# Layer A's o projection by pairs of heads: products of 512 moving columns instead of 256

## The chip, the cores and the metric

The kernel runs on 1 core of a Trainium2 chip. The metric is the device time of one execution in microseconds (us); before the change its median is 2071.47 us over 3 runs (2068.67 to 2078.06).

## The reference, cut to what matters

A trunk of two layers on a residual stream x of 1024 tokens by 1024 values, all in float32. Layer A is an mLSTM mixer, layer B dilated sliding-window attention. The change touches one product of layer A, the output gate `o_pre`, a third of the input projection:

```python
xm, z, o_pre = jnp.split(x @ w_in, 3, axis=-1)           # each 1024 x 2048
xc = jax.nn.silu(causal_dwconv(xm, conv_w, conv_b))
q, k, v = headwise(xc, wq), headwise(xc, wk), headwise(xm, wv)
gates = jnp.concatenate([q, k, v], axis=-1) @ w_if + b_if # i_pre, f_pre: 4 + 4 per token
h_tilde = mlstm_chunkwise(q, k, v, i_pre, f_pre)          # 4 heads of 512
h = jax.nn.sigmoid(o_pre) * h_tilde
y = (groupnorm(h) * gn_g + skip * xc) * jax.nn.silu(z)
x = layer_norm(ALPHA * x + y @ w_out)
```

## The kernel before, in words

**Precision.** A float32 operand is split in a high part (a cast to fp32r on ScalarE, L92) and a low part (a subtraction, L93, on VectorE or the engine passed as `l_eng`). `mm3` (L95 to L99) forms a product from three matmuls: high by high, high by low, low by high.

**Strassen.** Layer A's projections are 2x2 block products in Strassen's form (a variant of Winograd) with seven products in place of eight. The operands of x, `x["11"]`, `x["12"]`, `x["22"]` and the sums `s1` to `s4`, are made once (`operands`) and kept as high and low parts in slots 0 to 7 and 12 to 31. The weights come as four quarters b11, b12, b22, b21 (`quarters`, L177), from which sums are made in place (L243, L247, L260, L261). Results are sums of PSUM banks (`plus` L224, `result` L230).

**The o projection** (`layer_a_project`, L556 to L577) runs `strassen_steps` once for each of four heads. With `tokens` given, the activations are the stationary operand (128x128, 128 tokens) and the weights move, 256 columns in each matmul: one head has 512 columns, half of it is a block. A set of results, 512 tokens by 256 columns, takes two banks, so the four sets a, b, c, d take all eight. Each product splits its quarter in two halves of 128x512 and runs 2 x 4 x 2 x 3 = 48 matmuls. The order in one head is a (b11 by x11), a again (b21 by x12), the sums b12 and b11, b (by s2), u2 = u2 + b, c (by s3), u3 = u2 + c, d (by s1), c again (by x22), d again (by s4). c may be added to only after u3 has read it. `sigmoid` takes the tanh of each finished result (L570) into slots 38 and 39 and stores it in DRAM (L572). For head 0 the subtractions and sums of the weights are on GpSimd (`V if hd else G`), for the others on VectorE.

**Slots.** All large buffers in SBUF are numbered slots of 128 x 4 KB; a `Ring` hands them out in turn, and whoever asks for a slot waits for the last user of its former tile. In the o projection raw weights use 34, 35, 32, 33; split pairs 36, 37, 8, 9, 49, 47; u2 and u3 use 10, 11.

**Around it.** Ahead come the streams of xm and the z gates (`gates`, L453 to L459), with `values` (L521 to L530). `gate_tables` stands ahead of the o projection in the program: the rows `gs` (slot 47) go through four sets of small matmuls (L598, L600; two banks in turn), are copied by ScalarE (L602), and a chain of row operations follows, mostly on VectorE (L607 to L637). `columns()` (L647 to L651) comes after head 0. Behind it, `layer_a_attend` begins with `prep_q` (L686 to L692: a product with a block matrix loaded from `dA` to slot 48, through banks 6 and 7, then a split), `prep_v` (loads of v and casts, L679 to L681) and scores (banks 4 and 5). The xc rows are loaded (L581) into the slots that the operands s2, s3, s1, s4 of x leave free.

**Order.** The program is written as a dataflow. A planner puts it into one queue for each engine beforehand, from its own estimates of durations and with the program's order as priority; on the chip each queue runs strictly in that order. Nearly all DMAs are issued from one queue, SyncE's (SP).

Of the kernel before, what the change touches and what calls it, by code (L numbers as in the profile page):

```python
# [13 lines left out]
AF = mybir.ActivationFunctionType  # L14
ALU = mybir.AluOpType
# [3 lines left out]
P = 128  # L19
# [41 lines left out]
class Kernel:  # L61
# [123 lines left out]
    def strassen_steps(self, raw, x, banks, dest, done, eng, tokens=None, mid=None, early=False, second=False):  # L185
# [99 lines left out]
        yield  # L285
        result(0, 1, u2, d)

    def rstd(self, x, n, tag):

        v = self.nc.vector  # L290
        y = self.t(self.cp, [P, n], tag=tag + "y", bufs=4)
        w = self.t(self.cp, [P, n], tag=tag + "w", bufs=4)
        v.tensor_scalar(y.bitcast(I32), x.bitcast(I32), 1, -1,
                        op0=ALU.logical_shift_right, op1=ALU.bitwise_xor)
        v.tensor_tensor(y.bitcast(I32), y.bitcast(I32), self.magic[:, 0:n].bitcast(I32), op=ALU.add)
        for _ in range(3):
            v.tensor_tensor(w, y, x, op=ALU.mult)
            v.scalar_tensor_tensor(w, w, -0.5, y, op0=ALU.mult, op1=ALU.mult)
            v.scalar_tensor_tensor(y, w, 1.5, y, op0=ALU.add, op1=ALU.mult)
        return y  # L300
# [104 lines left out]
    def layer_a_project(self):  # L405
        nc, tc, a, cp = self.nc, self.tc, self.a, self.cp
        V, A, G, T = nc.vector, nc.scalar, nc.gpsimd, nc.tensor
# [3 lines left out]
        def load(half, kh, js=range(2)):  # L411
            for j in js:
# [3 lines left out]
        x = self.operands(raws, {"11": (0, 1, 2, 3), "12": (4, 5, 6, 7), "22": (12, 13, 14, 15), "s1": (16, 17, 18, 19),  # L416
                                 "s2": (20, 21, 22, 23), "s3": (24, 25, 26, 27), "s4": (28, 29, 30, 31)}, {})
# [135 lines left out]
        columns = self.gate_tables(gs, gx, pv)  # L553


        self.w_raw, self.w_hl, self.u_slots = Ring(34, 35, 32, 33), Ring(36, 37, 8, 9, 49, 47), Ring(10, 11)  # L556
        tos = Ring(38, 39)
        for hd in range(HA):
            to = {}

            def place(half, i):
                to[half, i] = t = self.slot(tos, (P, 2, 512))
                return [[(t[:, j], slice(0, P))] for j in range(2)]

            def sigmoid(half, i, aps):
                if (half, i) == (0, 0):
                    place(0, 0)
                t = to[half, i]
                for j in range(2):
                    A.activation(t[:, j], aps[j], AF.Tanh, scale=0.5)  # L570
                rows = self.dram["o", hd].rearrange("(h t p) (i n) -> h i p t n", h=2, p=P, i=2)[half, i]
                nc.sync.dma_start(rows, t.rearrange("p j (t n) -> p (j t) n", t=2))  # L572

            self.strassen(self.quarters(a["w_o"][hd]), x, ((0, 1), (2, 3), (4, 5), (6, 7)), place, sigmoid, V if hd else G,
                          tokens=lambda ap, t: ap[:, t * P:t * P + P])
            if hd == 0:
                columns()  # L577
        self.xc = []
        for c in range(NC_A):
# [858 lines left out]
def arrays_of(i):  # L1438

    c = np.ascontiguousarray  # L1440
    x = np.asarray(i["x"])[0]
    w_in = np.asarray(i["a_w_in"])[0]
    kv = np.asarray(i["b_w_kv"])
    w2 = np.asarray(i["b_w_in"])[0]
    coltile = lambda w: c(w.reshape(KD, P, -1, P).transpose(2, 1, 0, 3)).reshape(-1, P, KD * P)
    perch = lambda v: c(v.reshape(NC_A, P).T)
    r = {"x": x, "ln_g": np.asarray(i["ln_g"]), "ln_b": np.asarray(i["ln_b"])}

    def quarters(w):
        t = w.reshape(-1, 2, P, 2, 512)  # L1450
        return c(np.stack([t[:, 0, :, 0], t[:, 1, :, 0], t[:, 1, :, 1], t[:, 0, :, 1]], 1).reshape(
            -1, 2, 2, P, 512).transpose(0, 1, 3, 2, 4)).reshape(-1, 2, P, 1024)

    r["lnT"] = c(np.stack([r["ln_g"][0].reshape(KD, P).T, r["ln_b"][0].reshape(KD, P).T], 1))
    r["xq"] = c(x.T.reshape(4, 2, P, 2, 512).transpose(3, 0, 2, 1, 4)).reshape(2, 4, P, 1024)
    r["w_xm"] = quarters(coltile(w_in[:, 0:INNER]))
    r["w_z"] = quarters(coltile(w_in[:, INNER:2 * INNER]))
    wo = w_in[:, 2 * INNER:].reshape(2, 4, P, HA, 2, 256).transpose(3, 0, 4, 2, 1, 5).reshape(HA, 2, 2, P, 1024)
    r["w_o"] = np.stack([wo[:, 0, 0], wo[:, 0, 1], wo[:, 1, 1], wo[:, 1, 0]], 1)
    r["convw"] = c(np.asarray(i["a_conv_w"])[0].reshape(4, NC_A, P).transpose(2, 1, 0))  # L1460
    r["convb"] = perch(np.asarray(i["a_conv_b"])[0])
    for n in ("q", "k", "v"):
        r[f"w{n}T"] = c(np.asarray(i["a_w" + n])[0].transpose(0, 2, 1).reshape(NC_A, P, 4).transpose(1, 0, 2))
    rep = lambda w: c(np.repeat(w[:, None], 4, axis=1).reshape(NC_A, P, *w.shape[1:]).swapaxes(0, 1))
    r["wkr"] = rep(np.asarray(i["a_wk"])[0])
    r["wifr"] = np.stack([rep(w) for w in np.asarray(i["a_w_if"])[0].reshape(3, 512, 4, 8)])
    r["bif"] = c(np.asarray(i["a_b_if"])[0].reshape(2, 4).T)
    r["gng"] = perch(np.asarray(i["a_gn_g"])[0])
    r["skip"] = perch(np.asarray(i["a_skip"])[0])
    r["w_out"] = c(np.asarray(i["a_w_out"])[0].reshape(NC_A, P, D))  # L1470
    kvt = kv.reshape(KD, P, 3, 2, HB, P)
    wv = kvt[:, :, :, 1].reshape(2, 4, P, 3, 2, 2, 256).transpose(3, 4, 0, 5, 2, 1, 6).reshape(3, 2, 2, 2, P, 1024)
    r["w_v2"] = quarters(kvt[:, :, 2, 1].transpose(2, 1, 0, 3)).reshape(2, 2, 2, P, 1024)
# [37 lines left out]
```

## Time and profile before

| | |
|---|---|
| median of 3 runs | 2071.47 us |
| profiled execution | 2070.5 us, span 2068.7 us |
| PE (TensorE) busy | 2001.8 us, 97% |
| PEld (weight loads) busy | 1721.8 us, 83% |
| DVE (VectorE) busy | 1462.1 us, 71% |
| ACT (ScalarE) busy | 1003.1 us, 48% |
| POOL (GpSimd) busy | 188.9 us, 9% |

Times of rows are us from the start of the span. A row of a timeline is start, duration, engine, line, operation, output from input with shapes, count of merged instructions, and in brackets the engine's idle time before it with what ended it. Matmuls are pipelined: their durations overlap, so the cost of one in a stream is the distance between starts. A row of groups (by line and form) ends with busy time, mean ns of one, then the idle time ahead of them and what ended it. In a table of windows the columns are the stretch, its length, the busy time (and instructions) of PE, PEld, DVE, ACT and POOL, the granted clock of PE, the busy share of the DMA engines and GB/s.

### The profile page before, as it was taken

How to read it: one execution, taken by the hardware profiler on the slowest of the kernel's cores; microseconds unless marked ns; L12 is line 12 of the kernel's file. 1: busy time of each engine (PE TensorE's matmuls, PEld its weight loads, DVE VectorE, ACT ScalarE, POOL GpSimd, SP SyncE). 2: the span in 40 equal slices, each digit the busy share in tenths (PEclk: the TensorE clock that was granted, in tenths of full speed). 3: DMA queues.
4: the chain of work that ended last, by engine and by line, in shares of the span. 5: the costliest groups of instructions: out<-in, count | busy, mean ns of one | idle time of the engine just before them, and what ended most of it. 6: DMA issues, size and time to landing. Idle time of an engine off the chain costs nothing.

```text
span 2068.7 us, 29452 instructions
## 1 busy us (share of the span) xinstructions
PE 2001.8 (97%) x11008; PEld 1721.8 (83%) x11008; DVE 1462.1 (71%) x2825; ACT 1003.1 (48%) x1920; POOL 188.9 (9%) x145
## 2 busy tenths in 40 slices
PE   8989999999999999999999999999999999999997
PEld 6868888899888888877788898888888898888786
DVE  8787788465367767465678757766878757757878
ACT  5455555533745453343434536555534635655631
POOL 0230000600244443000000000000000000000000
PEclk9999999999999999999999999999999999999999
DMA  4455555443844643516113231122543132123753
GB/s 166 145 190 175 181 214 175 153 146 114 324 172 158 214 146 114 199 62 213 56 46 127 68 133 62 61 93 91 187 166 121 64 113 70 62 92 106 260 210 122
DMA packets 117046, 288.20 MB, mean 139 GB/s; under 512 B 13028, under 2 KB 43172, under 8 KB 116904
## 3 DMA queue, kind: packets, MB, share of 16 engines
q1 hardware_dynamic: 116904, 286.34, 39.2%
q8 instruction: 86, 1.41, 0.3%
q14 instruction: 56, 0.46, 0.1%
HBM read 200.00 MB, written 86.30 MB: 138 GB/s over the span
## 4 chain that ended last, share of the span: by engine, by line
PE 77%; DVE 11%; DMA 7%; ACT 2%; issue 2%; SPq 0%; DVEq 0%; ACTq 0%
PE b L97 24%; PE b L99 24%; PE b L98 24%; DVE s L93 3%; DMA s<-df 3%; PE b L521 1%; PE b L1159 1%; DMA s<-dv 1%; DVE s L141 1%; ACT s L92 1%; PE b L527 1%; PE b L788 1%; DVE s L1276 1%; DVE s L486 1%; DVE s L230 0%
## 5 line engine op out<-in xcount | busy, mean ns | idle before, releaser
L97 PE MATMUL b<-s,s 128*128 128x512 f32 (+2 forms) x3256 | 1125.4, 354 | 28.4 <-ACT s L92 16.7
L98 PE MATMUL b<-s,s 128*128 128x512 f32 (+2 forms) x3256 | 1140.6, 352 | 9.3 <-DVE s L93 9.3
L99 PE MATMUL b<-s,s 128*128 128x512 f32 (+2 forms) x3256 | 1125.1, 352 | 5.3 <-DVE s L93 5.1
L97 PEld LDWEIGHTS b<-s,s 128*128 128x128 f32 x3256 | 617.0, 190 | 117.4 <-ACT s L92 22.3
L92 ACT CAST s<-s 128x512 fp32r<-128x512 f32 (+4 forms) x674 | 435.1, 659 | 552.9 <-PE b L99 318.3
L98 PEld LDWEIGHTS b<-s,s 128*128 128x128 f32 x3256 | 619.7, 190 | 88.1 <-DVE s L93 10.7
L99 PEld LDWEIGHTS b<-s,s 128*128 128x128 f32 x3256 | 617.9, 190 | 88.5 <-DVE s L93 8.4
L93 DVE TENSOR_TENSOR s<-s,s 128x512 fp32r<-128x512 f32 (+3 forms) x656 | 500.9, 773 | 248.0 <-ACT s L92 245.4
L230 DVE TENSOR_TENSOR s<-s,b 128x512 f32<-128x512 f32 x192 | 130.5, 682 | 70.8 <-PE b L99 61.5
L224 DVE TENSOR_TENSOR s<-s,b 128x512 f32<-128x512 f32 x128 | 86.5, 680 | 26.6 <-PE b L99 25.9
L1146 ACT ACTIVATE s<-s,nmax 128x128 f32<-128x128 f32 (+1 forms) x192 | 84.5, 442 | 38.3 <-DVE nmax L1144 37.5
L93 DVE TENSOR_TENSOR s<-b,s 128x512 fp32r<-128x512 f32 (+1 forms) x96 | 59.0, 630 | 43.3 <-ACT s L92 43.0
L486 DVE SCALAR_TENSOR_TENSOR s<-s,c_convw,s 128x512 f32<-128x512 f32 (+3 forms) x96 | 74.8, 786 | 2.3 <-ACT s L483 1.8
L1142 DVE CUSTOM_DVE_ANT_0 s<-b,k 128x128 f32<-128x128 f32 (+1 forms) x192 | 57.8, 345 | 17.5 <-PE b L99 17.4
L243 DVE TENSOR_TENSOR s<-s,s 128x512 f32<-128x512 f32 (+1 forms) x55 | 41.6, 756 | 39.3 <-DMA s<-in_w_xm 13.9
L722 ACT ACTIVATE s<-s,k 128x128 f32<-128x128 f32 x144 | 46.9, 392 | 41.7 <-DVE s L93 19.3
L92 ACT CAST s<-b 128x512 fp32r<-128x512 f32 (+1 forms) x96 | 50.3, 545 | 31.8 <-PE b L99 19.7
L681 POOL TENSOR_TENSOR s<-s 128x512 fp32r<-128x512 f32 x32 | 43.3, 1369 | 161.6 <-DMA s<-dv 112.4
L93 POOL TENSOR_TENSOR s<-s,s 128x512 fp32r<-128x512 f32 x18 | 30.5, 1702 | 254.1 <-ACT s L92 253.2
L237 ACT COPY s<-b 128x512 f32<-128x512 f32 x64 | 37.4, 585 | 26.0 <-PE b L99 25.6
L792 POOL TENSOR_TENSOR s<-s,s 128x512 f32<-128x512 f32 x32 | 42.3, 1338 | 62.8 <-DVE s L791 47.9
L1095 ACT ACTIVATE s<-s 128x512 fp32r<-128x512 f32 x48 | 42.0, 882 | 11.8 <-DVE s L230 11.6
(178 smaller groups left out, 1448.4 us busy)
## 6 DMA issues: line engine op xcount, KB each, us to landing
s<-in_w_qk SPq DMA_DIRECT2D x48, 512.0 KB
s<-in_w_out SPq DMA_DIRECT2D x40, 512.0 KB
dp<-s SPq DMA_DIRECT2D x32, 512.0 KB
s<-dp SPq DMA_DIRECT2D x32, 512.0 KB
s<-in_w_z SPq DMA_DIRECT2D x24, 512.0 KB
s<-in_w_v SPq DMA_DIRECT2D x24, 512.0 KB
dg<-s SPq DMA_DIRECT2D x24, 512.0 KB
s<-dg SPq DMA_DIRECT2D x24, 512.0 KB
```

The costliest lines, as they stand in the source:

```text
L92: self.nc.scalar.copy(h, src)
L93: (l_eng or self.nc.vector).tensor_tensor(l, src, f(h), op=ALU.subtract)
L97: mm(ps, lh, rh, start=start, stop=False, skip_group_check=skip)
L98: mm(ps, lh, rl, start=False, stop=False, skip_group_check=skip)
L99: mm(ps, ll, rh, start=False, stop=stop, skip_group_check=skip)
L224: V.tensor_tensor(o, p, q, op=add)
L230: V.tensor_tensor(o, p[lane][rows], q[lane][rows], op=add)
L486: V.scalar_tensor_tensor(u[i][:, lo:o + 512], xm[i][:, lo - s:o + 512 - s], convw[:, c, 3 - s:4 - s], u[i][:, lo:o + 512], op0=ALU.mult, o ...
L681: G.tensor_tensor(l, f(l), f(h), op=ALU.subtract)
L722: A.activation(E[:, i * P:i * P + P], src[:, i * P:i * P + P], AF.Exp, bias=self.bias[:, hd, ig, j:j + 1])
L1142: V.tensor_tensor_reduce(out=dst, in0=sc, in1=bias, op0=ALU.add, op1=ALU.max, scale=1.0, scalar=-3e38, accum_out=mx[:, b:b + 1])
L1146: A.activation(res[b][0], res[b][0], AF.Exp, bias=nm[:, b:b + 1], accum_out=stat[:, 1, g, b:b + 1])
```

## The change

A new function, `strassen_wide`, does the seven products for two heads at once: a block is now 512 columns, a whole head, and a set of results takes four banks (one for each 128 tokens). The eight banks hold two sets, so b takes 4 to 7 after a has taken 0 to 3, c 0 to 3 again, d 4 to 7. A quarter of the weights is two slots of 1024; each product makes four splits of 128x512, for each of which four matmul triples of 512 columns run. The split pairs are four (36, 37, 49, 47), the raw quarters have fixed places (pair 0: 34, 35, 50, 51, 32, 33, 48, 52), u2 and u3 use 8 to 11. VectorE does the subtractions and sums of both pairs. The weights in DRAM are laid out anew on the host.

```diff
+    def strassen_wide(self, raw, x, banks, dest, done, eng):
+        b11, b12, b22, b21 = raw
+        banks = Ring(*banks)
+        new = lambda: [self.bank(i) for i in banks.next()]
+        u2, u3 = [[t[:, j] for t in [self.slot(self.u_slots, (P, 2, 512)) for _ in range(2)] for j in range(2)]
+                  for _ in range(2)]
+        def product(acc, w, xp, first):
+            for k in range(4):
+                wh, wl = self.pair(self.w_hl)
+                self.split(wh, wl, w[k // 2][:, k % 2 * 512:k % 2 * 512 + 512], eng)
+                xh, xl = [p[k // 2][:, k % 2] for p in xp]
+                for t in range(4):
+                    ts = slice(t * P, t * P + P)
+                    self.mm3(acc[t], xh[:, ts], xl[:, ts], wh, wl, first and k == 0, k == 3, skip=True)
+        def sums(o, p, q, op):
+            for j in range(2):
+                eng.tensor_tensor(o[j], p[j], q[j], op=op)
...
+        a = new()
+        product(a, b11, x["11"], True)
+        for o, p in zip(u2, a):
+            A.copy(o, p)
+        product(a, b21, x["12"], False)
+        done(0, 0, a)
+        sums(b12, b22, b12, sub)
+        sums(b11, b12, b11, add)
+        b = new()
+        product(b, b11, x["s2"], True)
+        plus(u2, u2, b)
+        c = new()
+        product(c, b12, x["s3"], True)
+        plus(u3, u2, c)
+        sums(b21, b21, b11, sub)
+        sums(b11, b22, b11, sub)
+        d = new()
+        product(d, b11, x["s1"], True)
+        result(1, 1, u3, d)
+        product(c, b21, x["22"], False)
+        result(1, 0, u2, c)
+        product(d, b22, x["s4"], False)
+        result(0, 1, u2, d)
...
-        self.w_raw, self.w_hl, self.u_slots = Ring(34, 35, 32, 33), Ring(36, 37, 8, 9, 49, 47), Ring(10, 11)
+        self.w_hl, self.u_slots = Ring(36, 37, 49, 47), Ring(8, 9, 10, 11)
         tos = Ring(38, 39)
-        for hd in range(HA):
+        places = (((34, 35), (50, 51), (32, 33), (48, 52)), ((50, 51), (48, 52), (34, 35), (32, 33)))
+        for pair in range(2):
+            raw = {}
+            for n in (0, 3, 1, 2):
+                kh, nh = ((0, 0), (0, 1), (1, 1), (1, 0))[n]
+                raw[n] = [self.slot(i) for i in places[pair][n]]
+                for j in range(2):
+                    nc.sync.dma_start(raw[n][j], a["w_o"][pair, kh, nh, j])
...
-            self.strassen(self.quarters(a["w_o"][hd]), x, ((0, 1), (2, 3), (4, 5), (6, 7)), place, sigmoid, V if hd else G,
-                          tokens=lambda ap, t: ap[:, t * P:t * P + P])
-            if hd == 0:
+            self.strassen_wide([raw[n] for n in range(4)], x, ((0, 1, 2, 3), (4, 5, 6, 7)), place, sigmoid, V)
+            if pair == 0:
                 columns()
```

## Rows read from the trace of the kernel before

**Rows 1.** The page: engines' busy time, and the last chain by line.

```profile
PE 2001.8 (97%) x11008; PEld 1721.8 (83%) x11008; DVE 1462.1 (71%) x2825; ACT 1003.1 (48%) x1920; POOL 188.9 (9%) x145
PE b L97 24%; PE b L99 24%; PE b L98 24%; DVE s L93 3%; DMA s<-df 3%; PE b L521 1%; PE b L1159 1%; DMA s<-dv 1%; DVE s L141 1%; ACT s L92 1%; PE b L527 1%; PE b L788 1%; DVE s L1276 1%; DVE s L486 1%; DVE s L230 0%
```

**Rows 2.** Windows of the o projection and of the stretch behind it.

```profile
390.00:412.40 22.40, 22.40 (x190) 22.40 (x188) 18.98 (x14) 12.82 (x17) 17.83 (x9) 1.00 0.31 95
415.00:418.40 3.40, 3.17 (x15) 3.20 (x16) 3.40 (x7) 0.00 (x0) 0.00 (x0) 0.50 0.63 245
418.40:550.40 132.00, 132.00 (x1107) 131.85 (x1107) 68.40 (x99) 64.15 (x110) 7.00 (x5) 1.00 0.51 173
555.70:561.80 6.10, 6.10 (x15) 5.07 (x16) 2.05 (x3) 2.21 (x5) 3.30 (x3) 0.50 1.03 413
```

**Rows 3.** PE's timeline: narrow matmuls in the stage, wide ones later, first and last.

```profile
449.74 0.28 PE L98 MATMUL b<-s,s 128*128 128x256 f32 x1
...
451.90 0.28 PE L98 MATMUL b<-s,s 128*128 128x256 f32 x1
...
899.70 0.39 PE L98 MATMUL b<-s,s 128*128 128x512 f32 x1
...
901.97 0.39 PE L99 MATMUL b<-s,s 128*128 128x512 f32 x1
```

**Rows 4.** PE's timeline: its two stops, and the end of the half speed.

```profile
415.23 0.55 PE L97 MATMUL b<-s,s 128*128 128x256 f32 x1 [2.55 <-DVE s L224]
...
418.50 0.28 PE L97 MATMUL b<-s,s 128*128 128x256 f32 x1
...
555.70 1.54 PE L97 MATMUL b<-s,s 128*128 128x512 f32 x3 [3.72 <-ACT s L92]
```

**Rows 5.** Groups by line and form, 371 to 450 us: low parts of weights.

```profile
L93 POOL TENSOR_TENSOR s<-s,s 128x512 fp32r<-128x512 f32 x12 | 21.3, 1784 | 14.0 <-ACT s L92 13.7 <-DVE s L230 0.4
...
L93 DVE TENSOR_TENSOR s<-s,s 128x512 fp32r<-128x512 f32 x12 | 8.1, 684 | 9.1 <-ACT s L92 9.0
```

**Rows 6.** DVE's timeline from 389 us: gate chain and o work.

```profile
389.96 0.84 DVE L607 TENSOR_SCALAR s<-s 4x1024 f32<-4x1024 f32 x1 [12.07 <-ACT s L602]
390.83 3.31 DVE L608 TENSOR_TENSOR s<-s,s 4x1024 f32<-4x1024 f32 x1
...
396.70 2.20 DVE L612 TENSOR_TENSOR s<-s,s 4x1024 f32<-4x1024 f32 x1
...
407.97 3.27 DVE L623 TENSOR_TENSOR_SCAN s<-s,s 4x1024 f32<-4x1024 f32 x1
...
414.42 1.26 DVE L224 TENSOR_TENSOR s<-s,b 128x512 f32<-128x512 f32 x2
...
418.73 1.20 DVE L628 TENSOR_TENSOR s<-s,s 4x1024 f32<-4x1024 f32 x1
...
420.59 1.21 DVE L243 TENSOR_TENSOR s<-s,s 128x1024 f32<-128x1024 f32 x1
```

**Rows 7.** PE's timeline: end of the z gates, last set of gate matmuls.

```profile
374.68 0.48 PE L99 MATMUL b<-s,s 128*128 128x512 f32 x1
...
387.23 1.02 PE L598 MATMUL b<-s,c_sel 16*4 16x512 f32 x2
388.17 1.04 PE L600 MATMUL b<-c_ident,gx 128*4 128x128 f32 x8
```

**Rows 8.** ACT's timeline from 372 us: casts that waited for a slot or load.

```profile
376.79 0.62 ACT L92 CAST s<-s 128x512 fp32r<-128x512 f32 x1 [0.24 <-DMA dz<-s]
...
385.43 1.04 ACT L92 CAST s<-s 128x1024 fp32r<-128x1024 f32 x1 [0.81 <-DMA s<-in_w_out]
...
388.28 0.62 ACT L92 CAST s<-s 128x512 fp32r<-128x512 f32 x1 [1.22 <-PE b L598]
```

**Rows 9.** Timelines of DVE and of ACT at the stage's end.

```profile
552.38 1.28 DVE L230 TENSOR_TENSOR s<-s,b 128x512 f32<-128x512 f32 x2 [6.82 <-DMA do<-s]
...
552.99 0.62 ACT L680 CAST s<-s 128x512 fp32r<-128x512 f32 x1 [2.95 <-DMA s<-dv]
```

**Rows 10.** SP's timeline: loads of the xc rows.

```profile
527.46 9.44 SPq L581 DMA_DIRECT2D s<-dc  x8
```

More of the change, by code (lines that the diff above doesn't have):

```diff
@@ L286, in strassen_steps, with plus, result @@
         result(0, 1, u2, d)
+    def strassen_wide(self, raw, x, banks, dest, done, eng):
+        V, A = self.nc.vector, self.nc.scalar
+        sub, add = ALU.subtract, ALU.add
+        b11, b12, b22, b21 = raw
[14 more added lines that the diff above has]
+                eng.tensor_tensor(o[j], p[j], q[j], op=op)
+        def plus(outs, ps, qs):
+            for o, p, q in zip(outs, ps, qs):
+                V.tensor_tensor(o, p, q, op=add)
+        def result(half, i, p, q):
+            o = dest(half, i)
+            plus(o, p, q)
+            done(half, i, o)
+        a = new()
[21 more added lines that the diff above has]
+        result(0, 1, u2, d)
     def rstd(self, x, n, tag):
@@ L553, in layer_a_project @@
         columns = self.gate_tables(gs, gx, pv)
-        self.w_raw, self.w_hl, self.u_slots = Ring(34, 35, 32, 33), Ring(36, 37, 8, 9, 49, 47), Ring(10, 11)
+        self.w_hl, self.u_slots = Ring(36, 37, 49, 47), Ring(8, 9, 10, 11)
         tos = Ring(38, 39)
-        for hd in range(HA):
+        places = (((34, 35), (50, 51), (32, 33), (48, 52)), ((50, 51), (48, 52), (34, 35), (32, 33)))
[6 more added lines that the diff above has]
+                    nc.sync.dma_start(raw[n][j], a["w_o"][pair, kh, nh, j])
             to = {}
             def place(half, i):
-                to[half, i] = t = self.slot(tos, (P, 2, 512))
-                return [[(t[:, j], slice(0, P))] for j in range(2)]
+                to[half, i] = [self.slot(tos, (P, 2, 512)) for _ in range(2)]
+                return [t[:, j] for t in to[half, i] for j in range(2)]
             def sigmoid(half, i, aps):
@@ L567, in sigmoid @@
                     place(0, 0)
[L568 to L572, printed above, removed]
-            self.strassen(self.quarters(a["w_o"][hd]), x, ((0, 1), (2, 3), (4, 5), (6, 7)), place, sigmoid, V if hd else G,
-                          tokens=lambda ap, t: ap[:, t * P:t * P + P])
-            if hd == 0:
+                rows = self.dram["o", 2 * pair + i].rearrange("(h j t p) n -> h j p t n", h=2, j=2, p=P)
+                for j, t in enumerate(to[half, i]):
+                    for k in range(2):
+                        A.activation(t[:, k], aps[2 * j + k], AF.Tanh, scale=0.5)
+                    nc.sync.dma_start(rows[half, j], t)
+            self.strassen_wide([raw[n] for n in range(4)], x, ((0, 1, 2, 3), (4, 5, 6, 7)), place, sigmoid, V)
+            if pair == 0:
                 columns()
@@ L1457, in arrays_of @@
     r["w_z"] = quarters(coltile(w_in[:, INNER:2 * INNER]))
-    wo = w_in[:, 2 * INNER:].reshape(2, 4, P, HA, 2, 256).transpose(3, 0, 4, 2, 1, 5).reshape(HA, 2, 2, P, 1024)
-    r["w_o"] = np.stack([wo[:, 0, 0], wo[:, 0, 1], wo[:, 1, 1], wo[:, 1, 0]], 1)
+    r["w_o"] = c(w_in[:, 2 * INNER:].reshape(2, 2, 2, P, 2, 2, 512).transpose(4, 0, 5, 1, 3, 2, 6)).reshape(
+        2, 2, 2, 2, P, 1024)
     r["convw"] = c(np.asarray(i["a_conv_w"])[0].reshape(4, NC_A, P).transpose(2, 1, 0))
```

## Prediction

> **What bounds the kernel now.** I began with the busy line of the page and the shares of the last chain [rows 1]: TensorE (PE) is busy 97% of the span and the three matmul lines of `mm3` make up some 72% of the chain. So an edit is worth what it does to the matmul stream, plus or minus what makes that stream wait. The windows [rows 2] then cut out the o projection. It begins beside the last z-gate product, near 375 us, and ends at 550.4. For the heads after the first (418.4 to 550.4) PE and the weight-load row are both full, 132.00 and 131.85 of 132 us, with VectorE (DVE) at 68.40 and ScalarE (ACT) at 64.15: PE alone is the limit there. In the first head two other engines carry load: DVE works on the gate tables, GpSimd (POOL) on head 0's subtractions.
>
> Third, the matmul timeline gives the price of a product by its width [rows 3]. 128x256: 18 steps from 449.74 to 451.90 us, 0.120 us each. 128x512, the same three lines with activations stationary and weights moving as the change has them: 10 steps from 899.70 to 901.97, 0.227 us each. Two narrow products cost 0.240 us, one wide 0.227.
>
> Fourth, PE's stops [rows 4]. There are two in the stage or at its end. At 415.23 PE had been idle 2.55 us for DVE's L224, the sum u3 = u2 + c, without which the next product may not add into c. The next 15 matmuls take 3.27 us where 15 x 0.120 = 1.80 is normal, at a granted clock of 0.50 (the lower level, 1.2 GHz) [rows 2]: 1.5 us more. Cost of the first stop 2.6 + 1.5 = 4.1 us. At 555.70, in the first steps of the attention, PE had been idle 3.72 us for an ACT cast, and 6.1 us at 0.50 follow [rows 2, 4], which cost half of themselves if PE was the limit in them, 3.0 us. Together 6.7 us.
>
> **The change part by part.**
>
> *Width.* 4 heads x 7 products x 48 matmuls = 1344 of 256 columns become 2 x 7 x 48 = 672 of 512. 1344 x 0.120 = 161.3 us against 672 x 0.227 = 152.5: **-8.8 us**, nearly all of it on the path, since PE is full there. Only the reading of the steps leaves play: 8.5 to 9.2.
>
> At 256 columns the weight-load row is as full as PE's [rows 2]. The Trainium skill, "TensorE: Matmul & The Clock Gate", section Back-to-back issue gap, gives N/2.4 + 2.5 ns for an isolated step, 109.2 and 215.8 ns, and warns that loads also set the step in a real stream. By that formula the change would be worth 672 x 2.6 ns = 1.7 us; by the rows, five times that.
>
> *Work of the other engines.* Casts, subtractions and sums stay equal in number: 56 splits of 128x512 (4 per product instead of 2), 16 sums of 128x1024, 32 tanh, 16 loads and 16 stores of 512 KB. The stores now write rows of 512 values instead of 256, so the queue is not longer. One thing moves: head 0 used POOL for 14 subtractions and 4 sums; now DVE does them, 14 x 0.684 + 4 x 1.21 = 14.4 us [rows 5, 6]. For pair 1 (half of all o work) that is nothing: DVE needs some 28 x 0.69 + 8 x 1.21 + 20 x 0.68 = 42.6 us in a pair of 76.2 us (336 x 0.227). What matters is pair 0.
>
> *The gate chain beside pair 0.* DVE's queue is strictly in order. It stood idle 12.07 us before L607 at 389.96 [rows 6], waiting for ACT's L602, which itself waits for the fourth set of gate matmuls on PE [rows 7]. From 390.0 to 412.4 it was busy 18.98 us with 14 instructions, of which two were o work [rows 2]. In the changed kernel subtractions of pair 0 lie in that queue too, before, between and behind the chain. In favour: the 12 idle us lie just there; L608 took 3.31 us beside a busy POOL, L628 of the same form 1.20 with POOL idle [rows 6], so with POOL silent the chain loses at least 2.1 us; and the wait that cost 4.1 us (u3 before c is used again) now has a product of 48 x 0.227 = 10.9 us between instead of 48 x 0.120 = 5.8. Against: the ring of split pairs shrinks from six to four, a look-ahead of 4 x 12 x 0.227 = 10.9 us instead of 6 x 24 x 0.120 = 17.3. From 390.0 to 412.4 DVE had 22.4 - 18.98 = 3.4 us free, with the 2.1 some 5.5; in that time, two products, it must now place 8 subtractions and 4 sums, 8 x 0.684 + 4 x 1.21 = 10.3 us. What lacks, 4.8 us, must go into the idle 12 us ahead of L607 or into the look-ahead. If neither takes any, PE stands 4.8 us and loses 1.5 at half speed after it, so I bound the new stop by 0 and 6 and take 2, nearer to 0 because the idle time is over twice the lack: **-2.1 us**, with -4.1 and +1.9 as ends.
>
> *Slots at the start.* Three buffers come free late, and the rows show when. Pair slot 49 is released by the z store (the cast at 376.79 waited for it), slot 47 holds the gate rows and is released by the last L598 (the cast at 388.28 waited for that) [rows 8]. In the new ring of four these are the third and the fourth quarter of the very first product; before, they were the fifth and sixth pair. So the first product cannot end before about 389.4 (cast 0.62, then DVE). Does PE have other work until then? The last z-gate matmul starts at 374.68 [rows 7]. From 375.0: three quarters of 36 x 0.227 = 8.2 us in all and four sets of gate matmuls of some 2.0 us: 16.2 us, to 391.2. The cover is 1.8 us, so I cost this at nothing; without the cover it is a rival below. Bank 3 is needed by the fourth token block of the first product and is released by the last z result at about 376; blocks one to three of two quarters (18 x 0.227 = 4.1 us) hide that.
>
> *Loads and SP's queue.* Eight loads per pair instead of four per head. Of pair 0's, slot 50 is the latest: a w_out load took it next in the kernel before, and the cast of that load had its data by 385.43 [rows 8]. The third product, which needs the sum made from it, starts near 406 less the look-ahead, 395: hidden, with 10 us to spare. Pushed out of their early places are two w_out loads, their first cast (1.04 us of ACT) and the load of the A matrix into slot 48; all are used only after the stage, and their slots come free with pair 1's middle products, over 20 us before its end. Zero.
>
> *The end of the stage.* The 3.72 us stop has its rows [rows 9]: DVE's last result waited for a store of o (6.82 us of idle), and ACT stood 2.95 us in L680, a cast of v values, for a DMA, with the q casts that PE needed queued behind it. Both were late because transfers were packed: the xc loads that start at 527.46 [rows 10] can go only as the operands s2, s3, s1, s4 fall free, within four short products of 5.8 us; DMA share 1.03 after 555.7 [rows 2]. With products of 10.9 us the same loads are spread over twice the time, and the v slots fall free 10.9 us before the end instead of under 6. What may be late next: the last product now holds banks 4 to 7, of which the first attention step needs 6 and 7 for q and 4, 5 for scores; DVE must add four banks (0.64 us each, two after the last matmul), and q goes through two banks in turns of matmul 0.7, cast 0.6, subtraction 0.7 [rows 5, 9]. PE then has about 2 to 4 us of short gaps but no single long one. Bounds: 1 us (everything spread, no drop of the clock) and 9 (the same stop plus the longer tail of banks). I take 4, against 6.7: **-2.7 us**, ends -5.7 and +2.3.
>
> *Sum.* -8.8 - 2.1 - 2.7 = -13.6 us. The profiled execution took 2070.5 us (span 2068.7); 2070.5 - 13.6 = 2056.9. The median of the runs, 2071.47, lies 1.0 above the profiled one: **2057.9 us**. Forecast's own range from the ends: -9.2 - 4.1 - 5.7 = -19.0 and -8.5 + 1.9 + 2.3 = -4.3, so 2052.5 to 2067.2.
>
> **The rivals.**
>
> A. *DVE becomes the bound in pair 0.* It takes over 14.4 us from POOL, and if L607 stands ahead of the subtractions in its queue the idle 12 us cannot be used; the splits then run behind the chain. For: the lack of 4.8 us above. Against: chain operations alternated with o work in the kernel before (L224 at 414.42 between chain steps). Price: a stop of 6 to 14 us, half speed included, in place of 4.1, so with 10: -8.8 + 5.9 - 2.7 = -5.6, 2065.9; span 2062 to 2071.
>
> B. *Slower: the first product hangs on slot 47.* Place: the fourth quarter of product one, pair 0. If its subtraction is queued behind L607 to L612 (389.96 to 398.9 [rows 6]), PE runs dry from 391.4 to 399.6, 8.2 us, followed by half speed (6.1 us, 3.0 lost, as after the 3.72 us stop), the splits of products two and three start late by the same (some 5 us more, in short stops), and the stop at L224 stays (no gain). With no gain at the end: -8.8 + 8.2 + 3.0 + 5 = +7.4, 2078.9. It decides once the first product is held back by over 9 us. For: waiting casts in the rows. Against: the cover of 1.8 us, and the data for that subtraction is there about 1 us before L607's.
>
> C. *The width gives nothing.* If a wide step took 0.240 us here, as two narrow ones, the change would not do what it says: 0, with both stops as forecast (-4.8), 2066.7. Against it stand the wide steps of 0.227 [rows 3]. By the formula of the Trainium skill cited above it would be 2065.0.
>
> D. *The order shifts elsewhere.* The order of every queue is worked out from the whole program, so later stages can change by a few us either way: 2050 or 2070.
>
> **How the numbers follow.** Forecast 0.58, A 0.21, B 0.12, C 0.04, D 0.05. What a measurement can tell from no change is 0.5%, 10.4 us: faster means under 2061.1, slower over 2081.8 at the far side, and B's 2078.9 reaches it only with a longer stop; I give half of B to each side. Nine tenths of the forecast lies under 2061.1 (0.52), and half of D: faster 0.55. Slower 0.06. The rest, A, C, half of B and of D and the forecast's edge, 0.39. The range leaves out B and D's low end: 2051 to 2071.
>
> **What would show it.** Matmuls of 128x512 at 0.227 us from about 375 us on, at half the count, with a weight-load row no longer full; no POOL work in the stage; DVE idle for less than 12 us before L607, and L608 near 1.2 us; no PE stop over 2 us between 390 and 440; the xc loads from about 500 us; no idle over 3 us and no clock of 0.50 after the stage. I am wrong if PE waits for L93 on DVE in the first 60 us of the stage (A, B), if the wide steps are over 0.23 us (C), or if the attention's first step starts with the same long stop.

## The result, and the profile after

The changed kernel takes 2060.24 us in the median of 6 runs (2057.94 to 2062.29). The kernel before, run beside it, took 2073.68 (2068.67 to 2078.06). The ratio is 0.9933, 95% interval 0.9920 to 0.9945: 13.4 us less, and more than the 0.5% that a measurement of this kernel can tell from no change. The prediction was 2057.9 us.

In the page of the changed kernel, first line and busy times, PE has 672 matmuls fewer and 9.8 us less work than in [rows 1], and POOL has 33.8 us less:

```profile
span 2058.5 us, 28088 instructions
PE 1992.0 (97%) x10336; PEld 1684.8 (82%) x10336; DVE 1468.4 (71%) x2843; ACT 1001.4 (49%) x1920; POOL 155.1 (8%) x127
```

The lines of the changed kernel carry other numbers: the matmuls of `mm3` are still L97 to L99 and the splits L92 and L93, but L598, L600, L602 and L607 are now L662, L664, L666 and L671 (L608 is L672, L612 L676, L623 L687), the sums of weights are L310, the tanh of o is L636, the xc loads L645. The windows of the changed kernel that answer to [rows 2], from the start of the o products to the first steps of the attention (columns as there):

```profile
371.40:390.00 18.60, 18.60 (x88) 11.21 (x87) 8.28 (x12) 6.26 (x12) 0.00 (x0) 1.00 0.48 161
390.00:412.40 22.40, 22.40 (x103) 18.34 (x102) 19.05 (x22) 16.68 (x24) 0.00 (x0) 1.00 0.13 48
412.40:535.00 122.60, 122.60 (x553) 101.42 (x552) 71.09 (x107) 63.41 (x111) 11.86 (x9) 1.00 0.60 206
535.00:560.00 25.00, 20.77 (x102) 16.50 (x101) 13.64 (x27) 15.73 (x33) 2.58 (x2) 1.00 0.69 239
```

PE is full from 371.4 to 535 us at full clock, the weight-load row no longer is (101.42 of 122.60 us), and POOL does nothing beside the gate chain. From 390.0 to 412.4 VectorE is busy 19.05 us, as in [rows 2], but with 22 instructions instead of 14. PE's timeline has the steps of the wide matmuls, and then the end of the stage, behind which all stops now lie (first and last of eleven rows; the last matmul of o, the first and the sixth of q in the attention, and the stops):

```profile
499.74 0.39 PE L97 MATMUL b<-s,s 128*128 128x512 f32 x1
...
502.00 0.39 PE L98 MATMUL b<-s,s 128*128 128x512 f32 x1
...
536.91 0.39 PE L99 MATMUL b<-s,s 128*128 128x512 f32 x1
537.14 0.39 PE L97 MATMUL b<-s,s 128*128 128x512 f32 x1
...
538.27 0.39 PE L99 MATMUL b<-s,s 128*128 128x512 f32 x1
541.00 0.90 PE L97 MATMUL b<-s,s 128*128 128x512 f32 x3 [2.34 <-ACT s L92]
...
546.68 0.68 PE L97 MATMUL b<-s,s 128*128 128x512 f32 x2 [1.59 <-ACT s L92]
...
548.68 0.67 PE L97 MATMUL b<-s,s 128*128 128x512 f32 x2 [0.19 <-ACT s L92]
```

Ten steps from 499.74 to 502.00 are 0.226 us each, as in [rows 3]. The stop at 415.23 of [rows 4] has gone. The stop of 3.72 us with half speed behind it has become three of 2.34, 1.59 and 0.19 us at full clock.

The end of o has to be counted here, because the matmuls of q have the same shape. In the narrow kernels 2688 matmuls of `mm3` lie ahead of the first wide one of the attention; with 672 fewer, number 2016 of the changed kernel is the one at 536.91. VectorE's last four sums of o, which need that matmul, agree: they are done at 538.02, before the matmul at 538.27 starts.

```profile
535.35 2.67 DVE L314 TENSOR_TENSOR s<-s,b 128x512 f32<-128x512 f32 x4 [6.09 <-PE b L99]
```

**Where the time went.** Single profiles differ in stretches that no edit touches: the part behind layer A's out projection took 1040.3 to 1047.6 us over all kernels here, and before's own profile has the low end of it. So the profiled spans differ by 10.2 us only (2068.7 and 2058.5), the medians by 13.4. I measured the changed part by itself, in three ways that the table below uses for every run:

- *steps*: the distances from each matmul of `mm3` to the next matmul's start, summed over the last 25 matmuls of the z gates and all of o, up to the first matmul of the attention. A stop counts in it.
- *end*: from there to the attention's first sum of weights (the first matmul with the ones).
- *stage*: from the last gate-weight matmul to that same sum; the expectations speak of this one. It also holds the small gate matmuls; in all fourteen profiles 22 z matmuls lie behind its start.

| kernel (profile) | steps | end | stage | ratio to before [95%] |
|---|---|---|---|---|
| before | 172.3 | 30.7 | 213.4 | |
| before, repeat (e4) | 171.0 | 29.4 | 210.8 | 1.0003 [0.999, 1.0017] |
| after | 159.6 | 29.2 | 199.1 | 0.9933 [0.992, 0.9945] |
| again_after | 159.6 | 28.4 | 198.3 | 0.9938 [0.9916, 0.996] |
| after, repeat (e8) | 159.5 | 27.3 | 197.2 | 0.9939 [0.9925, 0.9953] |
| e1_narrow | 168.2 | 27.7 | 206.2 | 0.998 [0.9965, 0.9995] |
| e2_before_dve | 168.2 | 29.4 | 208.0 | 0.9984 [0.9972, 0.9996] |
| e3_after_pool | 172.0 | 30.2 | 212.5 | 1.0006 [0.999, 1.0021] |
| e7_swap | 159.6 | 27.1 | 197.1 | 0.9929 [0.9909, 0.9949] |
| swap, repeat (e9) | 159.5 | 27.9 | 197.8 | 0.994 [0.9926, 0.9955] |
| e10_slot47_third | 160.6 | 27.3 | 198.3 | 0.9933 [0.9917, 0.9949] |
| e11_after_gated_xc | 159.6 | 29.8 | 199.6 | 0.9959 [0.9945, 0.9973] |
| e12_before_gated_xc | 171.0 | 25.7 | 207.0 | 1.0012 [0.9994, 1.003] |
| e13_swap_gated_xc | 159.5 | 31.4 | 201.3 | 0.9971 [0.9961, 0.9981] |

From before (mean 171.7) to after (mean 159.6) the steps give 12.1 us; the end gives 1.8 (30.1 to 28.3), and repeats of one kernel differ by as much there. Together that is 13.9, and the attention's first sum does come 14.3 us earlier (579.8 to 565.6, means); the time ahead of and between the two is 377.6 to 378.1 us in these five profiles.

### The profile page after: what moved, and what is told of

Read it like the earlier page. It is cut to its first block, busy times and chain, and to the rows that moved or that the text cites. A ratio compares the mean times of both kernels' runs of the same rounds, so it can differ in the third digit from the quotient of the medians.

```text
span 2058.5 us, 28088 instructions
## 1 busy us (share of the span) xinstructions
PE 1992.0 (97%) x10336; PEld 1684.8 (82%) x10336; DVE 1468.4 (71%) x2843; ACT 1001.4 (49%) x1920; POOL 155.1 (8%) x127
## 4 chain that ended last, share of the span: by engine, by line
PE 80%; DVE 9%; DMA 6%; issue 2%; ACT 2%; SPq 0%; DVEq 0%; ACTq 0%
PE b L98 25%; PE b L99 25%; PE b L97 25%; DMA s<-df 3%; DVE s L93 3%; PE b L578 1%; PE b L1223 1%; DVE s L141 1%; PE b L584 1%; PE b L852 1%; DVE s L1340 1%; ACT s L92 1%; DVE s L543 1%; DMA s<-in_w_xm 0%; DMA s<-dc 0%
## 5 line engine op out<-in xcount | busy, mean ns | idle before, releaser
L98 PE MATMUL b<-s,s 128*128 128x512 f32 (+3 forms) x3032 | 1102.1, 366 | 12.1 <-DVE s L93 12.0
L97 PE MATMUL b<-s,s 128*128 128x512 f32 (+2 forms) x3032 | 1082.6, 367 | 26.5 <-ACT s L92 18.3
L99 PE MATMUL b<-s,s 128*128 128x512 f32 (+3 forms) x3032 | 1086.9, 365 | 4.0 <-DVE s L93 3.9
L92 ACT CAST s<-s 128x512 fp32r<-128x512 f32 (+4 forms) x674 | 434.5, 659 | 550.4 <-PE b L99 316.1
L93 DVE TENSOR_TENSOR s<-s,s 128x512 fp32r<-128x512 f32 (+2 forms) x670 | 510.8, 772 | 243.2 <-ACT s L92 240.9
L97 PEld LDWEIGHTS b<-s,s 128*128 128x128 f32 x3032 | 573.6, 190 | 123.2 <-ACT s L92 23.0
L98 PEld LDWEIGHTS b<-s,s 128*128 128x128 f32 x3032 | 576.0, 190 | 100.1 <-DVE s L93 14.3
L99 PEld LDWEIGHTS b<-s,s 128*128 128x128 f32 x3032 | 574.1, 190 | 96.4 <-DVE s L93 7.6
L230 DVE TENSOR_TENSOR s<-s,b 128x512 f32<-128x512 f32 x168 | 114.2, 682 | 56.0 <-PE b L99 52.8
L224 DVE TENSOR_TENSOR s<-s,b 128x512 f32<-128x512 f32 x112 | 75.8, 680 | 25.2 <-PE b L99 24.8
L93 DVE TENSOR_TENSOR s<-b,s 128x512 fp32r<-128x512 f32 (+1 forms) x96 | 59.0, 630 | 45.7 <-ACT s L92 45.3
L92 ACT CAST s<-b 128x512 fp32r<-128x512 f32 (+1 forms) x96 | 50.2, 545 | 30.6 <-PE b L99 18.4
L1160 DVE SCALAR_TENSOR_TENSOR s<-s,s 128x512 fp32r<-128x512 f32 x48 | 42.2, 885 | 5.7 <-ACT s L1159 5.3
L1223 PE MATMUL b<-c_ident,s 128*128 128x128 f32 x280 | 44.8, 276 | 0.3 <-ACT s L1210 0.3
```

The lines of the kernel that those rows point to most:

```text
L92: self.nc.scalar.copy(h, src)
L93: (l_eng or self.nc.vector).tensor_tensor(l, src, f(h), op=ALU.subtract)
L97: mm(ps, lh, rh, start=start, stop=False, skip_group_check=skip)
L98: mm(ps, lh, rl, start=False, stop=False, skip_group_check=skip)
L99: mm(ps, ll, rh, start=False, stop=stop, skip_group_check=skip)
L224: V.tensor_tensor(o, p, q, op=add)
```

## Experiments

**Is it the width? One change undone.** The wide layout stays, with its slots, banks, loads and VectorE's work; each 512-column matmul triple becomes two of 256.

```diff
-                    self.mm3(acc[t], xh[:, ts], xl[:, ts], wh, wl, first and k == 0, k == 3, skip=True)
+                    for n in range(2):
+                        ns = slice(256 * n, 256 * n + 256)
+                        self.mm3(acc[t][:, ns], xh[:, ts], xl[:, ts], wh[:, ns], wl[:, ns],
+                                 first and k == 0 and n == 0, k == 3, skip=True)
```

> The changed kernel with each 512-column matmul of the o projection issued as two of 256 columns, on the same banks, slots, splits and queues. If the width is worth what the steps of the trace say (0.240 against 0.227 us), it is 8.8 us slower than the changed kernel, about 2069, some 5 us under the kernel before. If only a fixed cost per matmul were saved (2.5 ns by the skill's formula) it is 1.7 us slower, about 2062. If the gain came from buffers, banks and the freed GpSimd, it stays at 2060.

The changed kernel ran again beside it, as the measure on that chip:

> The changed kernel itself, unchanged, once more, so that the experiments of this group have it on the same chip, and to see in a second profile which part of the gain repeats. Expected: 12 to 15 us under the kernel before, no stop of PE in the o projection itself, some 4 us of stops in the attention's first step and no drop of the clock there. If the gain of the first profile (10 us) were luck of later stages, the second would show the stage's 14 us and another drift behind it.

Measured: 2071.68 us against 2064.79 for the changed kernel and 2076.51 for before on the same chip; steps 168.2 against 159.6 us. PE's timeline of the narrow kernel, first and last of fifteen rows:

```profile
499.79 0.28 PE L97 MATMUL b<-s,s 128*128 128x256 f32 x1
...
501.47 0.28 PE L99 MATMUL b<-s,s 128*128 128x256 f32 x1
```

14 steps in 1.68 us, 0.120 each. The width is worth 168.2 - 159.6 = 8.6 us in the steps (PE does not stop in o in either kernel), 6.9 between the medians and 0.998 - 0.9938 = 0.0042, some 8.7 us, between the ratios: two thirds of the change's gain, as [rows 3] said. Were it worth 1.7 us, this kernel would stand near 0.9946, below its interval.

**Why did the first stop go? Two theories.** The prediction's main reason was length: a longer product lies ahead of the one that waits for u3. The rival: GpSimd's work for head 0 lengthened the gate chain on VectorE, and with GpSimd silent the sum u3 comes in time whatever the length. The kernel before with only head 0's subtractions and sums moved to VectorE keeps the short product:

```diff
-                          ((0, 1), (2, 3), (4, 5), (6, 7)), place, sigmoid, V if hd else G,
+                          ((0, 1), (2, 3), (4, 5), (6, 7)), place, sigmoid, V,
```

> The kernel before with head 0's subtractions and sums on VectorE instead of GpSimd, nothing else. Theory 1, the first stop went because a product of 10.9 us instead of 5.8 lies between u3 and the next use of c: here the product is still 5.8 us, VectorE has 14.4 us more to do, so the stop of 4.1 us stays or grows, 0 to 6 us slower than before. Theory 2, it went because GpSimd no longer slows the gate chain: the chain is over 2 us shorter, the stop shrinks to 0 to 2 us, 2 to 4 us faster than before.

Measured: no stop from 370 to 540 us, steps 168.2 against before's 171.0 and 172.3, ratio 0.9984, some 3.3 us. The steps are those of the narrow kernel above, which has no stop either. VectorE's timeline in this kernel (numbered as before):

```profile
394.73 0.68 DVE L607 TENSOR_SCALAR s<-s 4x1024 f32<-4x1024 f32 x1
395.44 1.22 DVE L608 TENSOR_TENSOR s<-s,s 4x1024 f32<-4x1024 f32 x1
...
401.34 1.21 DVE L612 TENSOR_TENSOR s<-s,s 4x1024 f32<-4x1024 f32 x1
...
411.81 0.67 DVE L224 TENSOR_TENSOR s<-s,b 128x512 f32<-128x512 f32 x1
...
413.01 2.27 DVE L623 TENSOR_TENSOR_SCAN s<-s,s 4x1024 f32<-4x1024 f32 x1
...
417.16 0.91 DVE L625 MEMSET s<- 4x1024 f32 x1 [0.16 <-issue]
```

L608 takes 1.22 us instead of 3.31, L612 1.21 instead of 2.20, L623 2.27 instead of 3.27 [rows 6]. L607 starts 4.8 us later than in [rows 6]; 3.9 of these lie ahead of the chain (its last input, from L602, started at 393.17 instead of 389.25), the rest is subtractions that VectorE does first. PE never waits. So in the narrow kernel the product's length was not needed.

Why the sum is in time is shown only in part, because the edit changed two things. The rows of the chain are shorter, seven of them by 6.3 us in all; as an estimate, 6.3 us less would put before's u3 sums at 408.1 instead of 414.42, ahead of 412.7, where PE stopped for them. But the planner also gave VectorE another order: in [rows 6] the u3 sums (L224) stand behind the scan L623, here they stand ahead of it. Behind L625, as before, they would by the rows above have ended near 418.1, some 2.4 us after PE came to the product that needs them (415.72). No run keeps the old order with a silent GpSimd, so the shares of the two stay open.

The converse: the changed kernel with pair 0's subtractions and sums back on GpSimd, so the length is there and the silence is not.

```diff
-            self.strassen_wide([raw[n] for n in range(4)], x, ((0, 1, 2, 3), (4, 5, 6, 7)), place, sigmoid, V)
+            self.strassen_wide([raw[n] for n in range(4)], x, ((0, 1, 2, 3), (4, 5, 6, 7)), place, sigmoid, V if pair else G)
```

> The changed kernel with pair 0's subtractions and sums on GpSimd, as the kernel before had head 0's. From the run of the kernel before with VectorE alone, the first stop came from the gate chain, lengthened by GpSimd. Theory 2 (GpSimd lengthens the chain, whatever lies between): chain operations such as the first min return to 2 to 3 us, and GpSimd's own splits of 1.8 us, 28 of them and 8 sums, hold PE up; 3 to 8 us slower than the changed kernel, with a stop in its first 60 us. Theory 1 (the product of 10.9 us between u3 and the next use of c covers it): chain longer, but no stop, within 2 us of the changed kernel.

Measured: 2075.30 us against 2075.54 for before on that chip, ratio 1.0006. The whole gain is gone. Its groups on POOL from 364 to 470 us (with mean ns of one), PE's waits from 364 to 450 us (total, times, longest), the two windows at half clock behind its longest stops, rows of VectorE's chain, and ScalarE's rows ahead of the two longest stops:

```profile
L93 POOL TENSOR_TENSOR s<-s,s 128x512 fp32r<-128x512 f32 x28 | 40.1, 1441 | 258.1 <-PE b L578 224.9 <-ACT s L92 33.2
L310 POOL TENSOR_TENSOR s<-s,s 128x1024 f32<-128x1024 f32 x8 | 25.2, 3159 | 2.6 <-PE b L664 1.9 <-DMA s<-in_w_o 0.6
```

```profile
PE b L97 <- ACT s L92: 3.4, 1, 3.4
PE b L97 <- ACT s L324: 2.2, 1, 2.2
PE b L98 <- POOL s L93: 1.3, 3, 0.9
```

```profile
398.80:402.20 3.40, 3.32 (x8) 2.65 (x9) 3.37 (x2) 3.26 (x6) 3.40 (x2) 0.50 0.01 2
429.00:435.80 6.80, 5.90 (x14) 4.44 (x15) 2.16 (x4) 1.81 (x4) 4.97 (x4) 0.54 0.83 239
```

```profile
395.08 2.19 DVE L672 TENSOR_TENSOR s<-s,s 4x1024 f32<-4x1024 f32 x1
...
400.07 2.74 DVE L675 TENSOR_SCALAR s<-s 4x1024 f32<-4x1024 f32 x1
402.84 2.20 DVE L676 TENSOR_TENSOR s<-s,s 4x1024 f32<-4x1024 f32 x1
...
424.00 2.27 DVE L701 TENSOR_SCALAR gam<-gam,s 4x3 f32<-4x3 f32 x1
```

```profile
397.31 1.05 ACT L673 ACTIVATE s<-s 4x1024 f32<-4x1024 f32 x1 [1.91 <-DVE s L672]
398.27 1.99 ACT L324 COPY s<-b 128x512 f32<-128x512 f32 x4
...
427.43 1.06 ACT L693 ACTIVATE s<-s 4x1024 f32<-4x1024 f32 x1 [12.40 <-DVE s L692]
428.39 2.16 ACT L92 CAST s<-s 128x512 fp32r<-128x512 f32 x4
```

Stops of 3.4 + 2.2 + 1.3 = 6.9 us and half of some 10.2 us at half clock make 12.0; the steps grew by 172.0 - 159.6 = 12.4. The chain's rows stand at 2.2 to 2.7 us; the same rows of the changed kernel, beside a silent POOL, are these:

```profile
393.66 1.21 DVE L672 TENSOR_TENSOR s<-s,s 4x1024 f32<-4x1024 f32 x1
...
398.89 0.68 DVE L675 TENSOR_SCALAR s<-s 4x1024 f32<-4x1024 f32 x1
399.60 1.22 DVE L676 TENSOR_TENSOR s<-s,s 4x1024 f32<-4x1024 f32 x1
...
422.65 0.21 DVE L701 TENSOR_SCALAR gam<-gam,s 4x3 f32<-4x3 f32 x1
```

So the engine that the change gave up was the costly one for this work. The direction is shown both ways round. Its size is not one number: 2.8 to 4.1 us in the narrow kernel, 12.4 in the wide one, where GpSimd has 28 subtractions and 8 sums instead of 14 and 4. Only 1.3 us of the stops are waits for GpSimd's own subtractions. The other 5.6 come through ScalarE's queue: there the copies L324 stand behind L673, and four casts of weights behind L693, both of which wait for rows of the slowed chain. In the changed kernel these copies and casts run ahead of L673 and L693 (the copies from 393.20, L673 at 397.08; a cast at 421.77, L693 at 424.62). So the 12.4 us hold the planner's order as well as the slow rows.

And no stop of this kernel is a wait for u3, though GpSimd works and the chain is slow. The chain's last long row, L694, ends at 428.1, and the product of c, which u3 needs, at 441.2; without the 12.0 us of stops that would be 429.2, as an estimate, and PE comes to the product that waits for u3 only 10.9 us later. So in the wide kernel the length covers that wait, as the prediction had it.

**Does a buffer decide the first product?** Slot 47, released by the last gate matmuls, holds the fourth quarter of product one. Made the third quarter, it is needed four matmul triples, 2.7 us, earlier.

```diff
-        self.w_hl, self.u_slots = Ring(36, 37, 49, 47), Ring(8, 9, 10, 11)
+        self.w_hl, self.u_slots = Ring(36, 37, 47, 49), Ring(8, 9, 10, 11)
```

> The changed kernel with slot 47, which the gate rows hold until the last set of gate matmuls, as third instead of fourth of the split pairs. If the first product's cover is as reckoned (fourth quarter ready 1 to 2 us before PE runs out of other work), the third quarter must now wait until about 390 us while PE has only two quarters (5.4 us) and the gate sets (8 us) from 375: a stop of 1 to 3 us near 388, the stage that much longer. If the cover is much larger than reckoned, no stop and the time of the changed kernel.

Measured: one stop of 1.04 us, in PE's timeline of this kernel, and steps of 160.6 us, 1.0 more than after's; the ratio, 0.9933, can't tell it.

```profile
391.08 0.50 PE L98 MATMUL b<-s,s 128*128 128x512 f32 x1 [1.04 <-DVE s L93]
```

The cover in the changed kernel is thus, as an estimate, some 2.7 - 1.0 = 1.7 us, as the prediction reckoned (1.8), and the rival that hung on it did not come.

**What makes the stop at the stage's end? Banks or transfers.** The prediction had it that packed transfers cause the stop before, and that banks 4 to 7, held by the last product, set what is left after. First the banks: pair 1 takes its two sets the other way round, so that the attention's first banks come free one product earlier (the columns of the gate chain go to bank 0).

```diff
-            self.strassen_wide([raw[n] for n in range(4)], x, ((0, 1, 2, 3), (4, 5, 6, 7)), place, sigmoid, V)
+            self.strassen_wide([raw[n] for n in range(4)], x,
+                               ((4, 5, 6, 7), (0, 1, 2, 3)) if pair else ((0, 1, 2, 3), (4, 5, 6, 7)), place, sigmoid, V)
```

> The changed kernel with the two bank sets exchanged in pair 1 (4 to 7 first, 0 to 3 last; the transposes of the gate columns use bank 0), so that the banks of the attention's first step are free one product before the stage ends. If the 4 us of stops there come from banks that the last result holds, 2 to 4 us faster than the changed kernel, about 2057. If they come from ScalarE's queue, where casts of q stand behind tanh and behind scalings that wait for xc loads, no change, 2059 to 2061.

Measured: end 27.1 us, repeated 27.9, against 29.2, 28.4 and 27.3; ratio 0.9929, repeated 0.994. On the mean that is some 0.8 us, less than repeats differ by. The banks were not the limit; in the changed kernel too PE goes from the last matmul of o (536.91) to the first of q (537.14) without a stop.

Then the transfers. The first try moved 12 of the 16 xc loads to a later place in the program, in before, in after and in the exchanged kernel:

```diff
-            nc.sync.dma_start(self.xc[c], self.dram["xc", c])
+            if c < 4:
+                nc.sync.dma_start(self.xc[c], self.dram["xc", c])
...
+            if n in (1, 2, 3):
+                for c in range(4 * n, 4 * n + 4):
+                    nc.sync.dma_start(self.xc[c], self.dram["xc", c])
```

> The kernel before with 12 of the 16 xc loads issued four by four in the attention's second, third and fourth step instead of all at the end of the o projection. If packed transfers made the 3.72 us stop at the start of the attention and the drop of the clock behind it, both go: the stage up to the attention's first sum of weights gets 3 to 6 us shorter than before (213.4 us in the profile). If the stop comes from the turns of q through two banks, it stays.

> The changed kernel with the same 12 xc loads issued later. In its profile the q casts of the attention's first step stand behind scalings of xc that wait up to 3.4 us for their loads. If that makes the stops there, 1 to 3 us come off the stage (199.0 us), about 2058; if the loads only move the wait elsewhere, or the stops come from the tanh ahead of the casts, no change.

> The changed kernel with both: banks exchanged in pair 1 and 12 xc loads issued later. The exchange alone took 1 to 2 us off the stage in the profile. If the two causes add, all of the some 4 us of stops go: a stage of 195 us, 2 to 4 us under the changed kernel. If later stages give it back, the time stays within 2 us of the changed kernel.

All three came out in the very order of the kernels without the edit, in every queue: moving the loads in the program did not move them in the queue. They tell nothing on late loads and stand in the table as repeats.

The second try holds the same 12 loads back in SP's queue itself, behind the load of the next head's A matrix, in the same three kernels:

```diff
-            nc.sync.dma_start(f(At), self.dram["A", hd // 2][:, :, (hd % 2) * 512:(hd % 2) * 512 + 512])
+            self.at_load = nc.sync.dma_start(f(At), self.dram["A", hd // 2][:, :, (hd % 2) * 512:(hd % 2) * 512 + 512])
...
+            if n in (1, 2, 3):
+                for c in range(4 * n, 4 * n + 4):
+                    with self.tc.issue_after(self.at_load.ins):
+                        nc.sync.dma_start(self.xc[c], self.dram["xc", c])
```

> The kernel before with the same 12 loads held back. If packed transfers delayed the v loads and so the cast that stood ahead of the q casts, the stop of 3.7 us shrinks below 2 and the clock does not fall: stage 3 to 6 us shorter than the 210.8 to 213.4 of the kernel before, which would also be what the change gained there. If the v cast waits for its slot and not for the transfers, the stop stays near 3.7 us.

> The changed kernel with 12 of 16 xc loads held in the queue behind a load of the attention's next step, so that in ScalarE's queue no scaling of xc stands ahead of the q casts any more. If the scalings, which wait for their loads, make the stop of 2.7 to 4.1 us at the attention's start, the stop falls to about 2 us (four tanh of 0.6 us are still ahead) and the stage to 195 to 196 us. If the turns of q through two banks make it, the stage stays at 197 to 199 us.

> The changed kernel with the bank sets of pair 1 exchanged and the 12 loads held back: with the banks of q free one product early and nothing that waits for a load ahead of the casts. If both causes hold, the stop goes below 1 us and the stage to 194 us, 3 to 4 us under the changed kernel; if tanh of the last result stays ahead of the q casts in ScalarE's queue, it is no better than the loads alone.

Measured in the kernel before: its stop of 3.7 us becomes two short ones (PE's waits from 545 to 580 us), and the window from 550 to 576 us has no half speed left:

```profile
PE b L97 <- PE b L99: 1.0, 1, 1.0
PE b L97 <- ACT s L92: 0.5, 1, 0.5
```

```profile
550.00:576.00 26.00, 24.51 (x124) 20.47 (x122) 16.94 (x32) 16.25 (x35) 5.14 (x4) 1.00 0.66 221
```

The end falls to 25.7 us from 29.4 and 30.7: the xc loads were the cause before. In the kernel before, the DMA engines were full ahead of that stop, at a share of 1.02 from 527.4 to 551 us:

```profile
527.40:551.00 23.60, 23.60 (x197) 23.51 (x196) 7.27 (x12) 18.79 (x31) 0.00 (x0) 1.00 1.02 391
```

With 12 of the xc loads held back, the four v loads ahead of the stop are also issued earlier (the last at 544.88 instead of 548.67). Whether they were late before by that or by the full DMA engines, the run does not tell. The total does not move (1.0012): the loads are then late for the attention, which takes 236.1 us from its first to its last sum instead of 230.3 and 231.5, and in which PE waits 5.1 us for ScalarE's casts instead of 1.5 and 2.8. In the changed kernel the same edit costs: 2066.45 us, 0.9959. Its stop at the start shrinks to 0.56 us, and a new one of 3.14 us comes at 561.78 (ACT's timeline of that kernel, then PE's):

```profile
552.88 1.34 ACT L855 ACTIVATE s<-s,c_skip 128x512 f32<-128x512 f32 x2 [2.99 <-DMA s<-dc]
...
561.17 1.04 ACT L92 CAST s<-b 128x512 fp32r<-128x512 f32 x2
```

```profile
561.78 1.11 PE L97 MATMUL b<-s,s 128*128 128x512 f32 x3 [3.14 <-ACT s L92]
```

In ScalarE's queue scalings of xc rows stand ahead of the casts of q that PE needs; a scaling whose load is late holds the casts up. With that reading the changed kernel's own stops can be read too, in ScalarE's timeline there:

```profile
535.77 2.63 ACT L854 ACTIVATE s<-s,c_skip 128x512 f32<-128x512 f32 x4 [4.78 <-DMA s<-dc]
538.30 2.17 ACT L636 ACTIVATE s<-s 128x512 f32<-128x512 f32 x4
540.38 1.04 ACT L92 CAST s<-b 128x512 fp32r<-128x512 f32 x2
544.83 1.33 ACT L854 ACTIVATE s<-s,c_skip 128x512 f32<-128x512 f32 x2 [3.40 <-DMA s<-dc]
546.06 0.56 ACT L92 CAST s<-b 128x512 fp32r<-128x512 f32 x1
```

ScalarE stood 4.78 us for an xc load, then did four scalings and four tanh, 4.6 us, and only then the cast for which PE waited to 541.00. At 546.06 it is the same again. Whether the casts ahead of the scalings would take these stops away was not tried. The exchanged kernel with held-back loads was worse still (0.9971, one stop of 4.2 us). No version beat the changed kernel beyond the intervals.

## Why the prediction was right, point by point

**Total.** 2057.9 us forecast, 2060.24 measured; -13.6 us summed, -13.4 measured in the medians. The terms were not each as good as their sum: the first stop gave some 1.4 us more than forecast and the stage's end some 0.9 less, and that these nearly cancel is luck.

**Width: right.** -8.8 forecast, -8.6 by the steps. By the formula that the Trainium skill, "TensorE: Matmul & The Clock Gate", section Back-to-back issue gap, gives for an isolated matmul it would be 1.7 us. The measured steps, 0.120 and 0.226 us, decide against that figure here, where each matmul comes with its own weight load.

**First stop: right sign, too small, and half the reason.** -2.1 forecast; the stop went whole, 2.8 to 4.1 us by the steps, with nothing put in its place. That the longer product covers the wait for u3 held: no wait for it comes back in e3. But it was not the only way, for in e2 the stop goes without it. What I had too high was the new stop, bounded by 0 and 6 and put at 2 since VectorE took 14.4 us more work. I had counted GpSimd's interference only once, as the 2.1 us of L608, while L612 and L623 of [rows 6] carried 1.0 us each; against the same operations in e2 the seven two-input ones from L608 to L624 were 6.3 us longer in all. In the changed kernel VectorE waited 1.49 us ahead of the chain instead of 12.07, was busy as long as before from 390.0 to 412.4 with eight instructions more, and PE never stood still in o. The row of that wait, in VectorE's timeline there:

```profile
390.59 0.69 DVE L93 TENSOR_TENSOR s<-s,s 128x512 fp32r<-128x512 f32 x1 [1.49 <-ACT s L92]
```

Rival A, that VectorE becomes the bound, did not come; leaving the work on GpSimd would have cost 12.4 us in the wide kernel (e3).

**Stage's end: somewhat too large, and the wrong mechanism for the rest.** -2.7 forecast, -1.8 measured, with repeats that differ by up to 1.9. That the old stop came from the xc loads is shown by e12. Of what I named for the remainder, banks 4 to 7 are not it (e7), and q's turns through two banks had no run of their own; the rows put the stops down to ScalarE's queue, in which scalings wait for xc loads ahead of the casts. "No idle over 3 us" held; "no clock of 0.50" held in after's first profile and not in its second (again_after), where 3.5 us at 0.55 followed a stop of 2.92 us.

**Slots, loads, queue: right.** No stop in the first product, cover 1.7 us; the xc loads start at 488 us rather than near 525; for the loads of the third product's weights VectorE stood up to 2.49 us (at 384.75), PE never.

**Rivals.** A and B did not come, C is refuted by e1. D, an order that shifts elsewhere, does not show ahead of the attention: steps and end account for 13.9 of the 14.3 us by which its first sum comes earlier.

## What to carry to other kernels

Price matmul width by the distance between starts in the same kernel's own trace, with its weight loads; that was worth 8.6 us here, and the forecast of it was 0.2 us off. Before work is left on an "idle" GpSimd, compare rows of one form on VectorE with GpSimd busy and with it silent, for every operation of the chain beside it, and put that difference on GpSimd's bill; and look whether the edit also changed the order of a queue, as it did in e2 and e3. And when loads are packed at a stage's end, look at which in-order queue has a consumer of them ahead of the critical operation: here delaying the loads only moved the stop, and was paid back in the next stage.

## What the runs showed of the hardware

With GpSimd at work VectorE's operations took longer, some by a multiple of their own length: a 4x3 `tensor_scalar` took 2.27 us against 0.21, a 4x1024 one 2.74 against 0.68, two-input ones 2.19 against 1.21 (e3 against after). The Trainium skill, "SBUF — State Buffer", section Who interferes with whom, states that VectorE instructions with two SBUF inputs contend with GpSimd instructions that read SBUF, for ports that the two engines share under an exclusive lock, and that against VectorE's two-port modes whoever issues first has them for the whole instruction. These rows agree in kind: the loss does not scale with the instruction that loses (2.06 us for both `tensor_scalar`), and POOL's own are 1.4 to 3.2 us long.

What half speed follows was not regular: stops of PE of 2.34 and 2.68 us at the same place left the granted clock at 1.00, its upper level (after, and its repeat e8); one of 2.92 (again_after) and one of 1.93 us (the exchanged kernel's repeat, e9) were followed by some 3.5 us at 0.55 and 0.57, near the lower.
